# Feed-forward nets of a decoder trunk: gate, up and down by blocks with three matmuls a product, against two stages with two matmuls a product

## The chip, the cores and the metric

The kernel runs on one core of a Trainium2 chip. The metric is the time of one execution on the device in microseconds (us). Before the change the median of three runs is 920.85 us (920.54 to 921.05). The profiled execution spans 919.0 us from its first to its last instruction.

## What is computed

The reference is a decoder trunk in float32: 256 tokens of width 1024 go through two layers, each a feed-forward net (FFN), a mixer and another FFN. The even mixer is latent attention beside causal pooling, the odd one a gated spatial mixer.

```python
def _rmsnorm(x, g):
    xf = x.astype(jnp.float32)
    y = xf * lax.rsqrt(jnp.mean(xf * xf, axis=-1, keepdims=True) + EPS)
    return (y * g.astype(jnp.float32)).astype(x.dtype)

def _swiglu(x, w_gate, w_up, w_down):
    return (jax.nn.silu(x @ w_gate) * (x @ w_up)) @ w_down

...
    for layer in range(DEPTH):
        h = h + 0.5 * _swiglu(_rmsnorm(h, ffn_norm[layer, 0]), ffn_w_gate[layer, 0],
                              ffn_w_up[layer, 0], ffn_w_down[layer, 0])
        hn = _rmsnorm(h, mix_norm[layer])
...
        h = h + 0.5 * _swiglu(_rmsnorm(h, ffn_norm[layer, 1]), ffn_w_gate[layer, 1],
                              ffn_w_up[layer, 1], ffn_w_down[layer, 1])
```

The change concerns the four FFNs. Gate and up are 1024 x 2816 matrices, down is 2816 x 1024.

## The kernel before, in words

**Layout.** The residual `hT` lies with features on the partitions: 8 tiles of 128 features by 256 tokens. A product of an FFN is built with the weights as the stationary operand (128x128) and the 256 tokens moving.

**Split numbers.** TensorE multiplies in fp32r, so each float32 operand is split into a high half (rounded to fp32r) and a low half (the rest). A product takes three matmuls (`mm3`, lines 203 to 206): weights low times input high, weights high times input low, weights high times input high, all summed in one PSUM region. The input halves are two tiles, `xh` and `xl`; for the down projection they are `ph` and `pl`.

**Weight stream.** `chunks` lists all weights in the order of use, in pieces of 128 x 1024 floats (512 KB). SyncE (SP) loads each into a `raw` buffer (5 of them, line 157), ScalarE (ACT) casts it to `whi` (line 168), VectorE (DVE) subtracts to get `wlo` (line 176); there are 6 pairs of `whi` and `wlo`. `next_chunk` takes the next chunk and emits, ahead of the matmuls that use it, the casts and splits up to three chunks further on. All engines work their own instructions strictly in the order written here (a hand-written schedule), so what `next_chunk` emits stands on ACT and DVE behind everything emitted before it.

**An FFN (`ffn`, line 321).** The 2816 hidden features go in 11 blocks of 256. `gate_up(b)` uses four chunks of gate and up weights: for each of the 8 feature tiles k, four tiles of 128 outputs (two gate, two up), so 32 products of three matmuls. Two PSUM banks of 512 floats, G and U, hold two outputs each; they come from the rotating set of four `rot` banks. `epilogue` scales by the norm, applies Silu, multiplies, and splits the product into `ph` and `pl` (DVE lines 344, 347, 348, 352; ACT lines 345, 351). `down(b - 1)` then uses two chunks for the block before: 16 products, summed over all blocks into four `acc` banks that hold the eight output tiles of the FFN, two a bank. Gate/up of one block and down of the block before so alternate, six chunks a block.

**Norm.** The norm's factor is worked out beside the first block: `norm_sum` (a small matmul, then DVE line 275, then POOL, GpSimd) ahead of `gate_up(1)`, and `norm_row` (matmuls on lines 290 and 291, copies on lines 293 and 297) after two of its four chunks, followed by the epilogue of block 0.

**Handing over.** At a phase's end `finish` (line 305) adds each output tile to the residual (line 303, DVE), and makes the next phase's `xh` (line 253, ACT), `xl` (line 256, DVE) and squares (line 261, ACT; line 266, POOL). The next phase's matmuls begin as soon as the first of them is there.

**Extras in the first FFN.** After block 3 `early_loads` fetches small tensors; after block 6, behind the call of `down(5)`, `rope_tables` computes the rotary tables, about thirty small DVE instructions (lines 405 to 441) and one on ACT.

**The end.** In the last FFN the last two chunks go output tile by output tile, and each tile is added and sent out at once (line 395).

## Time and profile before

| what | value |
|---|---|
| median of the runs | 920.85 us |
| span of the profiled execution | 919.0 us |
| the profiled execution's own time | not listed apart from its span; the median of the runs lies 1.85 us above the span |
| TensorE matmuls | 7432, busy 909.8 us |
| VectorE busy | 577.4 us, 63% |
| ScalarE busy | 441.3 us, 48% |
| GpSimd busy | 96.9 us, 11% |
| read from HBM | 162.51 MB, 178 GB/s over the span |

The page gives busy time by engine, then the chain of work that ended last. In the rows of the timeline the first number is the start in us from the span's start, the second the duration. Matmuls are pipelined: a 128x256 matmul has a duration of 0.28 us, but the next one starts 0.12 us later, so what a matmul costs is the distance of the starts, not the duration. A row with "x4" merges four instructions, and a number in square brackets is the idle time of the engine ahead of it with what ended it.

### The profile page before, as it was taken

The page shows a single profiled execution, that of the slowest core. Times are in us where ns is not written, and L with a number is a line of the kernel's source. Part 1 is how long each engine was busy: PE and PEld are TensorE (multiplying, and loading weights), DVE is VectorE, ACT ScalarE, POOL GpSimd, SP SyncE. Part 2 cuts the span into 40 slices and gives each one's busy share as a digit, 9 for nine tenths or more (in the row PEclk, how much of TensorE's full clock was granted, in tenths as well). Part 3 has the DMA queues.
Part 4 walks back from the last instruction along what each step waited for, and adds up shares of the span by engine and source line. Part 5 has one row for each costly group of instructions (what it writes and reads, how often), then busy time and mean ns, then how long its engine had stood idle before and what let it go on. Part 6 is the DMA issues. An engine that isn't in the chain of part 4 may idle for free.

```text
span 919.0 us, 17791 instructions
## 1 busy us (share of the span) xinstructions
PE 909.8 (99%) x7432; PEld 899.8 (98%) x7432; DVE 577.4 (63%) x765; ACT 441.3 (48%) x606; POOL 96.9 (11%) x130
## 2 busy tenths in 40 slices
PE   8999999999999999999999999999999999999998
PEld 7999999999899999999999999999999999999998
DVE  7746576569876654654666654654858665564563
ACT  7535435457675543543554443543655554443441
POOL 4100000027523000000040000000220220000000
PEclk9999999999999999999999999999999999999999
DMA  8655645625353564464455464464446356356351
GB/s 279 230 194 192 223 139 192 222 103 178 111 165 117 198 226 172 157 227 167 160 208 184 151 234 166 154 229 168 151 176 204 126 196 245 143 186 226 139 183 47
DMA packets 48031, 164.70 MB, mean 179 GB/s; under 512 B 5456, under 2 KB 7760, under 8 KB 47952
## 3 DMA queue, kind: packets, MB, share of 16 engines
q1 hardware_dynamic: 47952, 163.58, 50.9%
q8 instruction: 58, 0.95, 0.4%
q14 instruction: 21, 0.17, 0.1%
HBM read 162.51 MB, written 1.05 MB: 178 GB/s over the span
## 4 chain that ended last, share of the span: by engine, by line
PE 96%; DVE 1%; POOL 1%; issue 1%; DMA 1%; SPq 0%; ACT 0%; DVEq 0%
PE rot L204 20%; PE rot L205 20%; PE rot L206 19%; PE acc L204 12%; PE acc L205 12%; PE acc L206 11%; DMA raw<-w_gu 1%; PE rot L942 0%; POOL diag L285 0%; DVE wlo L181 0%; PE rot L791 0%; PE rot L821 0%; PE acc L272 0%; PE rot L763 0%; DVE nb L800 0%
## 5 line engine op out<-in xcount | busy, mean ns | idle before, releaser
L204 PE MATMUL rot<-xh,wlo 128*128 128x256 f32 x1440 | 408.7, 284 | 1.8 <-DVE wlo L181 1.7
L205 PE MATMUL rot<-xl,whi 128*128 128x256 f32 x1440 | 407.3, 283 | 0.0
L206 PE MATMUL rot<-xh,whi 128*128 128x256 f32 x1440 | 407.2, 283 | 0.0
L168 ACT CAST whi<-raw 128x1024 fp32r<-128x1024 f32 (+2 forms) x303 | 305.6, 1044 | 177.9 <-PE rot L206 121.1
L176 DVE TENSOR_TENSOR wlo<-raw,whi 128x1024 fp32r<-128x1024 f32 (+2 forms) x298 | 350.2, 1226 | 42.1 <-ACT whi L168 41.9
L204 PEld LDWEIGHTS rot<-xh,wlo 128*128 128x128 f32 x1440 | 276.0, 192 | 2.9 <-DVE wlo L181 2.8
L205 PEld LDWEIGHTS rot<-xl,whi 128*128 128x128 f32 x1440 | 276.1, 192 | 0.0
L206 PEld LDWEIGHTS rot<-xh,whi 128*128 128x128 f32 x1440 | 276.0, 192 | 0.0
L204 PE MATMUL acc<-ph,wlo 128*128 128x256 f32 x704 | 198.0, 281 | 0.0
L205 PE MATMUL acc<-pl,whi 128*128 128x256 f32 x704 | 197.8, 281 | 0.0
L206 PE MATMUL acc<-ph,whi 128*128 128x256 f32 x704 | 197.6, 281 | 0.0
L344 DVE TENSOR_TENSOR t<-rot,rb 128x512 f32<-128x512 f32 x44 | 30.4, 690 | 193.9 <-PE rot L206 193.9
L206 PEld LDWEIGHTS acc<-ph,whi 128*128 128x128 f32 x704 | 132.8, 189 | 0.0
L205 PEld LDWEIGHTS acc<-pl,whi 128*128 128x128 f32 x704 | 132.8, 189 | 0.0
L204 PEld LDWEIGHTS acc<-ph,wlo 128*128 128x128 f32 x704 | 132.7, 188 | 0.0
L345 ACT ACTIVATE t<-t 128x512 f32<-128x512 f32 x44 | 27.8, 632 | 177.0 <-DVE t L344 177.0
L266 POOL TENSOR_TENSOR sqsum<-sq,sq 128x256 f32<-128x256 f32 x6 | 4.7, 778 | 529.6 <-ACT sq L261 529.6
L352 DVE TENSOR_TENSOR pl<-p,ph 128x512 fp32r<-128x512 f32 x44 | 30.5, 693 | 30.2 <-ACT ph L351 30.2
L351 ACT CAST ph<-p 128x512 fp32r<-128x512 f32 x44 | 27.3, 620 | 37.9 <-DVE p L348 37.9
L256 DVE SCALAR_TENSOR_TENSOR xl<-par_h,xh 128x256 fp32r<-128x256 f32 x48 | 30.4, 634 | 4.9 <-ACT xh L253 4.6
L348 DVE TENSOR_TENSOR p<-p,t 128x512 f32<-128x512 f32 x44 | 30.5, 693 | 4.8 <-ACT t L345 0.3
L253 ACT ACTIVATE xh<-par_h 128x256 fp32r<-128x256 f32 x48 | 24.3, 506 | 14.7 <-DVE par_h L303 11.6
(221 smaller groups left out, 748.5 us busy)
## 6 DMA issues: line engine op xcount, KB each, us to landing
raw<-w_gu SPq DMA_DIRECT2D x172, 512.0 KB, 4.8
raw<-w_down SPq DMA_DIRECT2D x88, 512.0 KB, 5.0
raw<-ew_out SPq DMA_DIRECT2D x8, 512.0 KB, 3.5
raw<-ow_v SPq DMA_DIRECT2D x8, 512.0 KB, 5.2
raw<-ow_u SPq DMA_DIRECT2D x8, 512.0 KB, 4.8
raw<-ow_out SPq DMA_DIRECT2D x8, 512.0 KB, 3.6
raw<-ew_p SPq DMA_DIRECT2D x4, 512.0 KB, 4.5
raw<-w_gu SPq DMA_DIRECT2D x7, 256.0 KB, 4.9
```

The source lines that it names most:

```text
L168: nc.scalar.copy(hi[:, :n], r[:, :n])
L176: eng.tensor_sub(lo[:, :n], r[:, :n], hi[:, :n].bitcast(F32))
L204: nc.tensor.matmul(out, wl, xh, start=start, stop=False, skip_group_check=True)
L205: nc.tensor.matmul(out, wh, xl, start=False, stop=False, skip_group_check=True)
L206: nc.tensor.matmul(out, wh, xh, start=False, stop=stop, skip_group_check=True)
L253: nc.scalar.activation(s.xh[:, k, :], hT[:, k, :], AF.Copy, scale=pcol(s.gname, s.goff + k))
L256: nc.vector.scalar_tensor_tensor(s.xl[:, k, :], hT[:, k, :], pcol(s.gname, s.goff + k), s.xh[:, k, :].bitcast(F32), op0=ALU.mult, op1=ALU. ...
L344: nc.vector.tensor_mul(t, bank3(G), bc(s.rb))
L345: nc.scalar.activation(t, t, AF.Silu)
L348: nc.vector.tensor_mul(p, p, t)
L351: nc.scalar.copy(ph, p)
L352: nc.vector.tensor_sub(pl, p, ph.bitcast(F32))
```

## The change

The weights of an FFN come in another order: all 44 chunks of gate and up, then all 22 of down. The FFN runs in two stages. The products of all blocks are kept in one SBUF tile `pp` (22 tiles of 128 features, low half and high half side by side).

The input's two halves lie side by side as well, in one tile `x`, low first. A product takes two matmuls (`mm2`): weights low times input high (256 columns), and weights high times both halves at once (512 columns). The result fills a whole bank of 512 floats: the first half holds the two small parts, the second the large one, and they have to be added afterwards.

`gate_up` therefore fills four banks a block instead of two; even blocks take the `acc` banks, odd ones the `rot` banks. A new step `evacuate` copies the first halves to SBUF (ACT) and adds the second halves (DVE), and `epilogue` works from SBUF. The down stage uses all eight banks, one for each output tile; the first three chunks are used for tiles 0 to 3 and then for 4 to 7, and the last two chunks go tile by tile in every FFN. Each tile is added to the residual in two steps (`add`), one for each half. The rotary tables are emitted behind `epilogue(6)`, as the code's order has it. The mixers still use three matmuls; their tiles only lie differently.

```diff
     def ffn_chunks(li):
         gu = [[w_gu[li, b, c] for c in range(4)] for b in range(NB)]
         dn = [[w_down[li, b, j] for j in range(2)] for b in range(NB)]
-        out = list(gu[0])
-        for b in range(1, NB):
-            out += gu[b] + dn[b - 1]
-        return out + dn[NB - 1]
+        return sum(gu, []) + sum(dn, [])
...
+    def mm2(bank, wh, wl, x, start, stop):
+        nc.tensor.matmul(bank[:, 0:T], wl, x[:, 1, :], start=start, stop=False, skip_group_check=True)
+        nc.tensor.matmul(bank, wh, x.rearrange("p s t -> p (s t)"), start=False, stop=stop,
+                         skip_group_check=True)
...
-        s.xh = xpool.tile([P, KD, T], F32R, tag="xh", name=nm("xh"), bufs=2)
-        s.xl = xpool.tile([P, KD, T], F32R, tag="xl", name=nm("xl"), bufs=2)
+        s.x = xpool.tile([P, KD, 2, T], F32R, tag="x", name=nm("x"), bufs=2)
+        s.xl, s.xh = s.x[:, :, 0, :], s.x[:, :, 1, :]
...
-    def finish(accs, nxt):
-        """h += acc; then the next phase's norm input."""
-        residual(accs, 0)
+    def finish(add, nxt):
+        add(0)
         for m in range(KD):
             norm_hi(nxt, m)
             if m + 1 < KD:
-                residual(accs, m + 1)
+                add(m + 1)
             norm_lo(nxt, m)
             norm_sq(nxt, m)
...
             def gate_up(b, hooks={}):
-                G, U = rot_bank(), rot_bank()
+                new = rot_bank if b % 2 else acc_bank
+                banks = [new() for _ in range(4)]
...
-                        for i, bank in enumerate((G, G, U, U)):
+                        for i, bank in enumerate(banks):
                             ms = slice(i * P, (i + 1) * P)
-                            mm3(bank3(bank)[:, i % 2, :], wh[:, kc, ms], wl[:, kc, ms],
-                                s.xh[:, k, :], s.xl[:, k, :],
-                                start=k == 0 and i % 2 == 0, stop=k == KD - 1)
-                return G, U
+                            mm2(bank, wh[:, kc, ms], wl[:, kc, ms], s.x[:, k], k == 0, k == KD - 1)
+                return banks
+
+            def evacuate(banks):
+                gu = fp.tile([P, 4, T], F32, tag="gu", name=nm("gu"))
+                a = fp.tile([P, 4, T], F32, tag="a", name=nm("a"), bufs=1)
+                for i, bank in enumerate(banks):
+                    nc.scalar.copy(a[:, i, :], bank[:, 0:T])
+                for i, bank in enumerate(banks):
+                    nc.vector.tensor_add(gu[:, i, :], bank[:, T:], a[:, i, :])
+                return gu
+
+            pp = fp.tile([P, 2 * NB, 2, T], F32R, tag="pp", name=nm("pp"), bufs=1)
...
-            gu0 = gate_up(0)
-            accs[0] = acc_bank()
+            gu0 = evacuate(gate_up(0))
+            bank = acc_bank()
...
             for b in range(1, NB):
-                gb = gate_up(b, {0: lambda: norm_sum(s, accs[0]), 2: mid} if b == 1 else {})
-                if b == 1:
-                    prev = later[0]
-                    for j in range(1, 4):
-                        accs[j] = acc_bank()
-                now = epilogue(*gb)
-                down(b - 1, *prev)
-                prev = now
+                gb = gate_up(b, {0: lambda: norm_sum(s, bank), 2: mid} if b == 1 else {})
+                epilogue(b, evacuate(gb))
                 if first and b == 3:
                     early_loads()
                 if first and b == 6:
                     rope_tables()
...
+            banks = [rot_bank() for _ in range(4)] + [acc_bank() for _ in range(4)]
+            K = 2 * NB
+
+            def down(k, m, w):
+                ms = slice(m * P, (m + 1) * P)
+                mm2(banks[m], w[0][:, 0, ms], w[1][:, 0, ms], pp[:, k], k == 0, k == K - 1)
+
+            def add(m):
+                for half in (banks[m][:, T:], banks[m][:, 0:T]):
+                    nc.vector.tensor_add(hT[:, m, :], half, hT[:, m, :])
+
+            ws = [next_chunk(1) for _ in range(3)]
+            for ms in (range(4), range(4, KD)):
+                for k in range(3):
+                    for m in ms:
+                        down(k, m, ws[k])
+            for k in range(3, K - 2):
+                w = next_chunk(1)
+                for m in range(KD):
+                    down(k, m, w)
+            ws = [next_chunk(1), next_chunk(1)]
+            for m in range(KD):
+                for j in range(2):
+                    down(K - 2 + j, m, ws[j])
+                if nxt is None:
+                    add(m)
+                    nc.sync.dma_start(outT[m], hT[:, m, :])
             if nxt is not None:
-                down(NB - 1, ph, pl)
-                finish(accs, nxt)
...
+                finish(add, nxt)
...
-            finish(accs, nxt)
+            finish(lambda m: residual(accs, m), nxt)
```

The first rows below are TensorE's (PE) at the start of FFN 1, where the even mixer's output projection ends and `gate_up(0)` begins, before the change. Names are out<-in with buffer numbers, then partitions x columns; `rot` and `acc` are PSUM banks; the words in brackets are the engines that the instruction waits for.

```order
L206 MATMUL acc_2877<-comb_h,whi_3165 128x256
L204 MATMUL rot_3482<-xh_2878,wlo_3249 128x256 [waits Activation_49]
L205 MATMUL rot_3482<-xl_2879,whi_3248 128x256 [waits DVE_49]
L206 MATMUL rot_3482<-xh_2878,whi_3248 128x256
L204 MATMUL rot_3482<-xh_2878,wlo_3249 128x256
L205 MATMUL rot_3482<-xl_2879,whi_3248 128x256
L206 MATMUL rot_3482<-xh_2878,whi_3248 128x256
L204 MATMUL rot_3483<-xh_2878,wlo_3249 128x256 [waits PE_49]
```

The same place on the same engine after the change:

```order
L203 MATMUL acc_2448<-comb,whi_2735 128x256
L207 MATMUL acc_3053<-x_2449,wlo_2819 128x256 [waits DVE_49,Activation_49]
L208 MATMUL acc_3053<-x_2449,whi_2818 128x512 [waits DVE_49]
L207 MATMUL acc_3054<-x_2449,wlo_2819 128x256 [waits DVE_49]
L208 MATMUL acc_3054<-x_2449,whi_2818 128x512
L207 MATMUL acc_3055<-x_2449,wlo_2819 128x256 [waits DVE_49]
L208 MATMUL acc_3055<-x_2449,whi_2818 128x512
L207 MATMUL acc_3056<-x_2449,wlo_2819 128x256 [waits DVE_49]
```

A product is now a 256 and a 512 wide matmul, and each of the four products of the first feature tile goes to an `acc` bank and waits for VectorE on its own, where before they went to `rot` banks and only the inputs were waited for.

The second place is VectorE (DVE) in the first FFN, where the rotary tables are computed. Before (`pl` is the last step of the epilogue of block 6, `wlo` the split of a weight chunk, `posi` the first step of the tables):

```order
L348 TENSOR_TENSOR p_1467<-p_1467,t_1464 128x512 [waits DVE_49,Activation_49]
L352 TENSOR_TENSOR pl_1471<-p_1467,ph_1470 128x512 [waits Activation_49]
L176 TENSOR_TENSOR wlo_1435<-raw_1316,whi_1434 128x1024 [waits DMAHW3_49]
L176 TENSOR_TENSOR wlo_1475<-raw_1348,whi_1474 128x1024 [waits DMAHW4_49,Activation_49]
L405 CAST posi_1534<-pos_i 128x2
```

After (`pp` is the last step of the epilogue of block 6):

```order
L355 TENSOR_TENSOR gu_987<-gu_987,rb_388 128x512 [waits DVE_49]
L357 TENSOR_TENSOR gu_987<-gu_987,rbh_390 128x512 [waits DVE_49]
L358 TENSOR_TENSOR gu_987<-gu_987 128x512 [waits DVE_49,Activation_49]
L361 TENSOR_TENSOR pp_212<-gu_987,pp_212 128x2x256 [waits Activation_49]
L419 CAST posi_1003<-pos_i 128x2
```

The two splits that stood between the epilogue and the tables are gone from there: the next split (`wlo_966`, the chunk of the last quarter of `gate_up(7)`) now stands behind the whole of the tables.

More of the change, by code (lines that the diff above doesn't have):

```diff
@@ L342, in epilogue @@
+            def epilogue(b, gu):
                 bc = lambda r: r.unsqueeze(1).to_broadcast([P, 2, T])
-                t = fp.tile([P, 2, T], F32, tag="t", name=nm("t"))
-                nc.vector.tensor_mul(t, bank3(G), bc(s.rb))
+                t, p = gu[:, 0:2, :], gu[:, 2:4, :]
+                nc.vector.tensor_mul(t, t, bc(s.rb))
                 nc.scalar.activation(t, t, AF.Silu)
-                p = fp.tile([P, 2, T], F32, tag="p", name=nm("p"))
-                nc.vector.tensor_mul(p, bank3(U), bc(s.rbh))
+                nc.vector.tensor_mul(p, p, bc(s.rbh))
@@ L348, in epilogue @@
                 nc.vector.tensor_mul(p, p, t)
-                ph = fp.tile([P, 2, T], F32R, tag="ph", name=nm("ph"))
-                pl = fp.tile([P, 2, T], F32R, tag="pl", name=nm("pl"))
-                nc.scalar.copy(ph, p)
-                nc.vector.tensor_sub(pl, p, ph.bitcast(F32))
-                return ph, pl
-            def down(b, ph, pl):
-                for j in range(2):
-                    w = next_chunk(1)
-                    for m in range(KD):
-                        out_tile(accs, m, w, (ph[:, j, :], pl[:, j, :]), b == 0 and j == 0,
-                                 b == NB - 1 and j == 1)
@@ L362, in ffn @@
-            gu0 = gate_up(0)
-            accs[0] = acc_bank()
-            later = []
+                out = pp[:, 2 * b : 2 * b + 2]
+                nc.scalar.copy(out[:, :, 1, :], p)
+                nc.vector.tensor_sub(out[:, :, 0, :], p, out[:, :, 1, :].bitcast(F32))
+            gu0 = evacuate(gate_up(0))
+            bank = acc_bank()
             def mid():
                 norm_row(s, half=True)
-                later.append(epilogue(*gu0))
-            prev = None
+                epilogue(0, gu0)
@@ L719, in even_mixer @@
             steps23 = window_sums((2, 3), nc.vector)
[L722 to L723 removed]
+            comb = xpool.tile([P, KD, 2, T], F32R, tag="x", name="comb", bufs=2)
+            cl, ch = comb[:, :, 0, :], comb[:, :, 1, :]
             def pool_mix(c, bank):
@@ L913, in odd_mixer @@
             u_sb = ot([P, KD, T], "u_sb")
-            zh = xpool.tile([P, KD, T], F32R, tag="xh", name="z_h", bufs=2)
-            zl = xpool.tile([P, KD, T], F32R, tag="xl", name="z_l", bufs=2)
+            zz = xpool.tile([P, KD, 2, T], F32R, tag="x", name="zz", bufs=2)
+            zl, zh = zz[:, :, 0, :], zz[:, :, 1, :]
             mixed, zs = {}, {}
@@ L981, in odd_mixer @@
             nxt = norm_begin(*nxt_args)
-            finish(accs, nxt)
+            finish(lambda m: residual(accs, m), nxt)
         return nxt
```

12 lines of the change are left out of this document (removed).

## The prediction

> **What bounds the kernel now.** I read the page's busy times and its chain first, then TensorE's waits, then long windows inside the four FFNs.
>
> ```profile
> PE 909.8 (99%) x7432; PEld 899.8 (98%) x7432; DVE 577.4 (63%) x765; ACT 441.3 (48%) x606; POOL 96.9 (11%) x130
> PE 96%; DVE 1%; POOL 1%; issue 1%; DMA 1%; SPq 0%; ACT 0%; DVEq 0%
> ```
>
> ```profile
> PE rot L204 <- DVE wlo L181: 1.7, 4, 0.7
> PE acc L290 <- POOL diag L285: 1.2, 1, 1.2
> ```
>
> ```profile
> 30.00:200.00 170.00, 170.00 (x1426) 170.00 (x1425) 104.53 (x139) 74.10 (x89) 1.66 (x2) 1.00 0.53 188
> 285.00:475.00 190.00, 190.00 (x1594) 190.00 (x1593) 114.22 (x128) 85.06 (x105) 10.28 (x14) 1.00 0.51 181
> 475.00:655.00 180.00, 180.00 (x1505) 179.76 (x1504) 105.07 (x117) 78.66 (x93) 6.00 (x9) 1.00 0.54 189
> 735.00:915.00 180.00, 180.00 (x1511) 180.00 (x1510) 102.43 (x114) 73.30 (x82) 4.70 (x7) 1.00 0.49 172
> ```
>
> TensorE (PE) is the chain, and it hardly waits. The windows' columns are length, then busy time and count for PE, weight loads, DVE, ACT and POOL, then the granted clock (1.00). In 720 us there are 6036 matmuls; some two in each window only straddle its edge, so 720/6028 = 119.4 ns a matmul of 256 columns. Whatever shortens the matmul stream shortens the kernel, and any wait on PE now lengthens it.
>
> **The pair against the triple.** A 512 wide matmul with its own weight load is in the trace twice: first and last of 96 in the odd mixer, first and last of 12 in the even one.
>
> ```profile
> 653.49 0.40 PE L204 MATMUL rot<-whi,xl 128*128 128x512 f32 x1
> 675.03 0.39 PE L206 MATMUL rot<-whi,xh 128*128 128x512 f32 x1
> ```
>
> ```profile
> 215.96 0.39 PE L204 MATMUL acc<-whi,ckvl 128*128 128x512 f32 x1
> 218.52 0.39 PE L206 MATMUL acc<-whi,ckvh 128*128 128x512 f32 x1
> ```
>
> 21.54/95 = 226.7 ns and 2.56/11 = 232.7 ns. I take 226.7: a long stream beside DMA, like the FFN's. Doubling the columns adds 107 ns, so about 12 ns of each matmul depend on no column, and the change drops one of three such parts: 3 x 119.4 = 358.3 becomes 119.4 + 226.7 = 346.1, 12.2 ns less (6.2 with 232.7). There are 4 x (352 + 176) = 2112 products. The first 48 lie where PE waits for others anyway (below), so 2064 x 12.2 = **25.2 us gained**, at the least 12.8.
>
> [...]
>
> **Work added beside PE.** A block of gate/up now has four copies on ACT and four adds on DVE more.
>
> ```profile
> 101.68 0.69 DVE L344 TENSOR_TENSOR t<-rot,rb 128x512 f32<-128x512 f32 x1 [5.57 <-PE rot L206]
> 105.19 5.76 DVE L176 TENSOR_TENSOR wlo<-raw,whi 128x1024 fp32r<-128x1024 f32 x5
> L303 DVE TENSOR_TENSOR par_h<-acc,par_h 128x256 f32<-128x256 f32 x48 | 19.6, 418 | 15.5 <-PE acc L206 15.5
> 481.89 0.37 ACT L293 COPY rb<-acc 128x256 f32<-128x256 f32 x1 [3.89 <-PE acc L291]
> raw<-w_gu SPq DMA_DIRECT2D x172, 512.0 KB, 4.8
> ```
>
> An epilogue takes 3.5 us (101.68 to 105.19), a split 1.15. From the end of a block's matmuls: last copy 0.6 us, adds to 1.05, epilogue to 4.6, four splits to 9.2. A block of PE is 32 x 0.346 = 11.1 us, so DVE has 1.9 us to spare. The first split behind the epilogue is done at 5.8 and needed after three chunks, at 8.3. On ACT the casts of the next chunks stand behind the copies and Silu, and begin at about 4.1; the first of them is wanted by the split at 5.8. SP issues a load when the split before it in that buffer is done, so four loads go out between 5.8 and 9.2 and land 4.8 us later; their casts come behind the next block's epilogue, after 15. So in the steady stage the extra work costs nothing; without the 1.9 us of cover, every microsecond more on DVE would cost PE one in each of 40 blocks (rival 2). At the start of down the twelve products on the `rot` banks (4.2 us) cover the evacuation of the `acc` banks. DMA moves the same bytes, and the number of splits is the same.
>
> **Rotary tables.** Here the cover is gone.
>
> ```profile
> 118.87 0.69 DVE L344 TENSOR_TENSOR t<-rot,rb 128x512 f32<-128x512 f32 x1 [5.57 <-PE rot L206]
> 122.37 2.35 DVE L176 TENSOR_TENSOR wlo<-raw,whi 128x1024 fp32r<-128x1024 f32 x2
> 124.64 0.16 DVE L405 CAST posi<-pos_i 128x2 f32<-128x2 int32 x1
> 130.79 4.62 DVE L176 TENSOR_TENSOR wlo<-raw,whi 128x1024 fp32r<-128x1024 f32 x4
> ```
>
> The tables hold DVE for 6.15 us (124.64 to 130.79). Before, two splits stood ahead of them. Now they follow epilogue 6 directly: 4.6 + 6.15 + 1.2 = 12.0 us until the split of the last chunk of gate_up(7) is done, and PE wants it at 8.3: **3.7 us lost**.
>
> **The banks at a phase's start.** `gate_up(0)` used to take `rot` banks, which were free. Its four `acc` banks are now those in which the phase before left its result, and each is free only when DVE has added it to the residual. After a mixer the last two tiles share a bank, so the fourth product waits for tile 7.
>
> ```profile
> 273.99 0.28 PE L204 MATMUL rot<-xh,wlo 128*128 128x256 f32 x1
> 277.71 0.41 DVE L303 TENSOR_TENSOR par_h<-acc,par_h 128x256 f32<-128x256 f32 x1
> 725.53 0.28 PE L204 MATMUL rot<-xh,wlo 128*128 128x256 f32 x1
> 729.24 0.41 DVE L303 TENSOR_TENSOR par_h<-acc,par_h 128x256 f32<-128x256 f32 x1
> ```
>
> The even mixer's tile 7 is added at 278.12; with 0.06 for the signal the fourth product ends at 278.53, against 273.99 + 4 x 0.346 = 275.37: 3.15 us. The odd one is the same (730.06 against 726.91): **6.3 us for the two**. Later feature tiles are ready by then.
>
> Between FFN 1 and FFN 2 each tile has its own bank and takes two adds, the second waiting for the first.
>
> ```profile
> 462.28 0.51 ACT L253 ACTIVATE xh<-par_h 128x256 fp32r<-128x256 f32 x1 [2.91 <-DVE par_h L303]
> 462.82 0.48 DVE L256 SCALAR_TENSOR_TENSOR xl<-par_h,xh 128x256 fp32r<-128x256 f32 x1 [0.25 <-ACT xh L253]
> 465.73 0.41 DVE L303 TENSOR_TENSOR par_h<-acc,par_h 128x256 f32<-128x256 f32 x1
> 466.06 0.63 DVE L256 SCALAR_TENSOR_TENSOR xl<-par_h,xh 128x256 fp32r<-128x256 f32 x1
> 466.61 0.41 DVE L303 TENSOR_TENSOR par_h<-acc,par_h 128x256 f32<-128x256 f32 x1
> ```
>
> Starts follow each other at 0.33 (add to `xl`) and 0.55 us (`xl` to add); a dependent add I put at 0.45 (0.42 and the signal; bounds 0.42 and 0.52). So 1.33 us a tile. Counted from the time tile 0 is summed, DVE has added tiles 4, 5, 6 and 7 at 5.55, 6.9, 8.25 and 9.6; PE, which by then runs tile by tile at 2 x 0.346, could begin the next FFN at 4.6. Its fourth product ends at 10.0 instead of 6.0: **4.0 us lost**. After FFN 0 and FFN 2 the mixers begin on the early `rot` banks; only a split behind the longer `finish` comes later.
>
> ```profile
> 206.71 0.43 PE L205 MATMUL rot<-wlo,xh 128*128 128x416 f32 x1
> ```
>
> That matmul already starts 0.27 us late in the even mixer; `finish` will end 6.1 instead of 5.6 us after the mixer's start: **0.5 us lost**.
>
> **The norm's wait, and the ends.**
>
> ```profile
> 18.09 1.75 DVE L176 TENSOR_TENSOR wlo<-raw,whi 128x1024 fp32r<-128x1024 f32 x1
> 20.30 0.16 DVE L275 TENSOR_SCALAR me<-acc 128x2 f32<-128x2 f32 x1 [0.46 <-PE acc L272]
> 27.37 0.39 PE L290 MATMUL acc<-diag,ones_r 128*128 128x256 f32 x1 [1.25 <-POOL diag L285]
> ```
>
> `norm_sum` now takes the bank of the first product of `gate_up(0)`, and L275 stands behind the four adds. In FFN 0 the split runs to 19.84, the adds follow, L275 moves from 20.3 to 21.2 and POOL's chain with it: L290 comes **0.9 us later**, and until there PE's gain is swallowed (the 48 products). In the other FFNs the same chain misses PE by some 0.15 us: **0.5 us for three**.
>
> ```profile
> 915.17 0.28 PE L206 MATMUL acc<-ph,whi 128*128 128x256 f32 x1
> 915.48 0.43 DVE L303 TENSOR_TENSOR par_h<-acc,par_h 128x256 f32<-128x256 f32 x1 [0.28 <-PE acc L206]
> ```
>
> At the very end the last add is done 0.45 us after PE. Two adds a tile (0.79) are slower than PE's 0.69 a tile, so DVE falls behind by 0.7 and has one add more: 1.55 us after PE, **1.1 us lost**.
>
> **The sum.** Lost: 3.7 + 6.3 + 4.0 + 0.5 + 0.9 + 0.5 + 1.1 = 17.0 us. Gained: 25.2. The span goes from 919.0 to 910.8; the median lies 1.85 above the span, so **912.6 us**, 0.9% faster. A measurement of this kernel can tell about 0.2% (1.8 us) from no change.
>
> **Rivals.**
>
> (1) *The wide matmul is dearer, slower than before.* If the 512 wide matmul beside the FFN's load costs what the twelve at 215.96 cost, the gain is 12.8, less 17.0: span 923.2, time 925.1. It turns at 25.2 - 17.0 = 8.2 us over 2064 products, 4.0 ns more than 226.7. For it: those twelve ran beside busy DVE, ACT and POOL. Against: the four windows run beside a busy DVE and ACT too and vary by less than 1 ns. Chance 0.14. [...]
>
> (2) *VectorE becomes the bound of gate/up.* If its block takes 11.5 us (operands that lie apart, waits for ACT), 0.4 us in each of 40 blocks is 16 us: 928.6. For it: only 1.9 of 11.1 us are spare. Against: all durations are those of the same shapes. Chance 0.08.
>
> (3) *The clock drops in the new pauses.* Should PE work at half speed for as long as a pause lasted (four pauses of some 3.7 us), it loses 4 x 1.85 = 7.4 us: 920.0. The windows grant 1.00, but show no such pause. Chance 0.06. [...]
>
> (4) *The pauses are shorter.* If PE's waits for the banks overlap with waits that I counted apart, or adds follow faster, and half of the 17.0 remains: 904.1. Chance 0.07.
>
> **Chances and range.** The forecast has 0.65; its own range, from the bounds of the dependent add and 1.5 ns either way on the pair, is 909 to 917. The range that should hold 8 in 10 takes in (3) and (4) in part and the near half of (1): 907 to 924. Faster by over 0.2%: the forecast, (4) and a little of (1): 0.73. Within 0.2%: the near edge of (1) and (3): 0.09. Slower: 0.18.
>
> **What would show it.** In the profile after: 256 and 512 wide matmuls following each other at 119 and 227 ns; PE waiting some 3.7 us for `wlo` once near 98 us (28.6 plus 25 chunks of 2.77); waits of the first products of FFN 1, 2 and 3 for L390 or L303 of 3 to 4 us in sum each; no wait of PE for `wlo` in other blocks. The forecast is wrong if the 512 wide matmul takes 231 ns or more, if PE waits in every block, or if the clock row falls below 1.00.

## The result, and the profile after

The changed kernel takes 927.61 us (median of 6 runs, 922.17 to 932.35) where the kernel before takes 920.64 beside it (6 runs, 920.11 to 921.05): ratio 1.008, 95% interval 1.0063 to 1.0098. It is 0.8% slower; 912.6 us, 0.9% faster, was forecast. The profiled execution took 928.45 us, its span is 926.3. One execution of an experiment below, e2_banks, took 3221.06 us at full clock; nothing on record says why, and it is left out of that median and range.

The head of the page after, with the granted clock in 40 slices and the chain:

```profile
span 926.3 us, 13892 instructions
PE 903.3 (98%) x5320; PEld 793.7 (86%) x5320; DVE 649.3 (70%) x973; ACT 498.2 (54%) x782; POOL 98.9 (11%) x130
PEclk9999999999998999999989999999999999999999
PE 88%; DVE 7%; POOL 1%; ACT 1%; issue 1%; DMA 1%; SPq 0%; DVEq 0%; POOLq 0%; ACTq 0%
```

There are 2112 matmuls fewer, as the change says, but PE is busy only 6.5 us less, and two slices of the clock row are no longer 9. What PE waited for (sum in us, times, longest; rows of under 0.4 us and three that are as before left out):

```profile
PE acc L207 <- DVE par_h L306: 4.5, 4, 1.1
PE rot L207 <- DVE wlo L173: 3.3, 1, 3.3
PE acc L207 <- DVE par_h L390: 3.1, 4, 0.9
PE acc L207 <- DVE wlo L178: 2.5, 4, 1.4
PE acc L293 <- POOL diag L288: 1.5, 1, 1.5
PE acc L275 <- DVE gu L347: 0.4, 1, 0.4
```

Three of them are new and are those that the prediction named: for the split behind the rotary tables (L173), for the mixers' results in the banks (L306), for FFN 1's results (L390). The waits for L178 all lie in the first 19 us, where the kernel before has 1.7 us of them. No block of the steady stage waits for VectorE. What was not forecast shows behind each wait. PE's rows at the end of the tables' pause:

```profile
101.38 0.58 PE L207 MATMUL rot<-x,wlo 128*128 128x256 f32 x1 [3.25 <-DVE wlo L173]
101.76 0.63 PE L208 MATMUL rot<-x,whi 128*128 128x512 f32 x1
102.40 0.63 PE L208 MATMUL rot<-x,whi 128*128 128x512 f32 x1
103.04 0.63 PE L208 MATMUL rot<-x,whi 128*128 128x512 f32 x1
103.68 0.63 PE L208 MATMUL rot<-x,whi 128*128 128x512 f32 x1
104.31 0.39 PE L208 MATMUL rot<-x,whi 128*128 128x512 f32 x1
```

Four pairs stand 0.64 us apart before they go back to 0.35. The windows there and behind the handing over to FFN 1 (columns as in the prediction; the granted clock is the third figure from the right):

```profile
101.00:102.00 1.00, 0.62 (x2) 0.62 (x3) 1.00 (x2) 1.00 (x2) 0.00 (x0) 0.50 0.00 0
103.00:104.00 1.00, 1.00 (x5) 0.90 (x4) 1.00 (x2) 0.00 (x0) 0.00 (x0) 0.50 1.07 381
105.00:106.00 1.00, 1.00 (x8) 0.88 (x7) 0.81 (x3) 1.00 (x4) 0.00 (x0) 1.00 0.93 352
277.00:278.00 1.00, 0.62 (x2) 0.30 (x2) 1.00 (x3) 0.94 (x3) 0.92 (x2) 1.00 0.00 0
279.00:280.00 1.00, 0.97 (x3) 0.87 (x4) 0.95 (x2) 0.99 (x3) 0.92 (x2) 0.50 0.00 0
284.00:285.00 1.00, 1.00 (x5) 0.81 (x5) 0.94 (x1) 0.00 (x0) 0.00 (x0) 0.50 0.83 336
286.00:287.00 1.00, 1.00 (x8) 0.88 (x7) 0.00 (x0) 0.35 (x1) 0.00 (x0) 1.00 0.96 373
```

The clock is 0.50 from 100.86 to 104.27 us behind the tables and from 278.35 to 285.17 behind the handing over, long after PE has work again. The same is seen at FFN 2 (469.49 to 476.32) and FFN 3 (735.74 to 739.15).

These edges, read from the granted clock of narrow windows, show when the clock falls. Its four falls, at 100.86, 278.35, 469.49 and 735.74 us, lie 177.49, 191.14 and 266.25 us apart, which is 52, 56 and 78 times 3.413 us; the half clock lasts 3.41 us behind the first and the last and 6.82 and 6.83 us behind the others, once and twice 3.413. So all eight edges of this execution lie on one grid of 3.413 us. These are the four grid windows that end with a fall (the second figure is PE's busy time in them):

```profile
97.44:100.86 3.42, 0.69 (x4) 0.32 (x3) 2.89 (x16) 2.28 (x4) 0.00 (x0) 1.00 0.00 0
274.94:278.35 3.41, 1.71 (x8) 0.75 (x6) 3.41 (x9) 3.25 (x9) 3.11 (x4) 1.00 0.11 41
466.08:469.49 3.41, 1.37 (x5) 0.59 (x4) 3.31 (x9) 2.20 (x6) 1.45 (x2) 1.00 0.00 0
732.32:735.74 3.42, 1.61 (x7) 0.65 (x5) 3.42 (x9) 3.26 (x9) 3.10 (x5) 1.00 0.00 0
```

PE was busy in them for 0.69 to 1.71 of 3.41 us, about half of the window at most.

The second surprise is the pair itself, a product's narrow and wide matmul; its spacing is the distance from one wide matmul's start to the next. Starts of wide matmuls in FFN 1, from gate/up and from down:

```profile
300.05 0.40 PE L208 MATMUL rot<-x,whi 128*128 128x512 f32 x1
379.78 0.40 PE L208 MATMUL acc<-x,whi 128*128 128x512 f32 x1
```

```profile
410.06 0.39 PE L208 MATMUL acc<-pp,whi 128*128 128x512 f32 x1
459.87 0.40 PE L208 MATMUL acc<-pp,whi 128*128 128x512 f32 x1
```

The first two are 230 pairs apart: 346.7 ns a pair. The other two are 141 apart: 353.3 ns. A pair has two spacings, and each stands unchanged through a stage or a large part of it. Both are means: the single steps alternate, 0.35 and 0.34 us in the first stretch, 0.35 and 0.36 in the second. Counted over all starts, 1148 pairs of this execution stand at 346.7 ns, 912 at 353.3, and 51 lie beside waits or at half clock (some expectations below count by whole stages, which gives 880 for the 912).

### The profile page after: what moved, and what is told of

Its sections match the earlier page's. It is cut to its first block, busy times and chain, and to the rows that moved or that the text cites. A ratio compares the mean times of both kernels' runs of the same rounds, so it can differ in the third digit from the quotient of the medians.

```text
span 926.3 us, 13892 instructions
## 1 busy us (share of the span) xinstructions
PE 903.3 (98%) x5320; PEld 793.7 (86%) x5320; DVE 649.3 (70%) x973; ACT 498.2 (54%) x782; POOL 98.9 (11%) x130
## 4 chain that ended last, share of the span: by engine, by line
PE 88%; DVE 7%; POOL 1%; ACT 1%; issue 1%; DMA 1%; SPq 0%; DVEq 0%; POOLq 0%; ACTq 0%
PE acc L208 27%; PE rot L208 24%; PE acc L207 14%; PE rot L207 12%; PE acc L202 2%; PE acc L201 2%; PE acc L203 2%; DVE par_h L390 2%; DVE x L259 2%; PE rot L202 1%; PE rot L203 1%; PE rot L201 1%; DMA raw<-w_gu 1%; DVE wlo L173 1%; DVE par_h L306 1%
## 5 line engine op out<-in xcount | busy, mean ns | idle before, releaser
L173 DVE TENSOR_TENSOR wlo<-raw,whi 128x1024 fp32r<-128x1024 f32 (+2 forms) x298 | 353.8, 1229 | 102.0 <-ACT whi L165 101.9
L208 PE MATMUL acc<-x,whi 128*128 128x512 f32 x768 | 275.3, 401 | 0.0
L207 PE MATMUL acc<-x,wlo 128*128 128x256 f32 x768 | 219.0, 285 | 10.4 <-DVE par_h L306 4.5
L208 PE MATMUL rot<-x,whi 128*128 128x512 f32 x640 | 225.4, 396 | 0.0
L207 PE MATMUL rot<-x,wlo 128*128 128x256 f32 x640 | 179.3, 280 | 3.3 <-DVE wlo L173 3.3
L208 PEld LDWEIGHTS acc<-x,whi 128*128 128x128 f32 x768 | 147.5, 192 | 34.0
L207 PEld LDWEIGHTS acc<-x,wlo 128*128 128x128 f32 x768 | 148.0, 193 | 15.1 <-DVE par_h L306 6.7
L208 PEld LDWEIGHTS rot<-x,whi 128*128 128x128 f32 x640 | 120.7, 189 | 28.2
L208 PE MATMUL acc<-pp,whi 128*128 128x512 f32 x352 | 127.3, 396 | 0.0
L208 PE MATMUL rot<-pp,whi 128*128 128x512 f32 x352 | 127.3, 396 | 0.0
L207 PEld LDWEIGHTS rot<-x,wlo 128*128 128x128 f32 x640 | 121.1, 189 | 3.6 <-DVE wlo L173 3.6
```

Source lines behind the costliest of these rows:

```text
L173: eng.tensor_sub(lo[:, :n], r[:, :n], hi[:, :n].bitcast(F32))
L207: nc.tensor.matmul(bank[:, 0:T], wl, x[:, 1, :], start=start, stop=False, skip_group_check=True)
L208: nc.tensor.matmul(bank, wh, x.rearrange("p s t -> p (s t)"), start=False, stop=stop, skip_group_check=True)
```

## The experiments

Theory: the waits are worth what was forecast; the rest is (a) half clock outlasting four pauses and (b) pairs at 353.3 ns. Rivals: the pauses alone cost more than they were priced at; the wide matmul is dear by what runs beside it. Where matmuls of zeros are added, they are extra work. A kernel is set against the kernel before on the same chip (median 920.17 to 920.46 there).

### One pause moved: e1_tables

```diff
-                if first and b == 6:
-                    rope_tables()
...
+                if first and k == 8:
+                    rope_tables()
```

The second place is in the down loop, where DVE has time (it is busy for 24.14 of the 50 us from 145 to 195 us in the changed kernel).

> The changed kernel, with the rotary tables emitted behind the ninth chunk of the first FFN's down stage instead of behind the epilogue of block 6. Theory (pauses and the clock they bring down): the pause of 3.4 us near 98 us and the stretch of half clock behind it (2.7 us at half speed, 1.4 us lost) both go, so about 5 us less than the changed kernel: some 922 to 923 us, and three stretches of half clock remain. Rival (the low clock is not the pauses' doing): only the 3.4 us go and a stretch of half clock remains near 100 us: 924 us.

Measured: 921.77 us (919.46 to 926.22), ratio 1.0018 (1.0007 to 1.003). The wait for L173 is gone, the clock stays at 1.00 there, and the other waits and their three stretches of half clock stay (the mean clock is 0.992):

```profile
PE acc L207 <- DVE par_h L306: 4.5, 4, 1.1
PE acc L207 <- DVE par_h L388: 3.1, 4, 0.9
```

The median is 5.8 us below the changed kernel's, where the pause was priced at 3.7; the half clock behind it (four pairs 0.29 us late, 1.2) would go with it. As the runs of this kernel scatter by 7 us and those of the changed kernel by 10, this alone proves no size.

### The banks: e2_banks, e3_both

```diff
-                new = rot_bank if b % 2 else acc_bank
+                new = acc_bank if b % 2 else rot_bank
-            bank = acc_bank()
+            bank = rot_bank()
-            for ms in (range(4), range(4, KD)):
+            for ms in (range(4, KD), range(4)):
```

e2_banks has this alone, so `gate_up(0)` starts on the banks that are free early; e3_both has it and the moved tables.

> The changed kernel with the two sets of banks exchanged: even blocks of gate/up take the rotating banks, odd ones the accumulator banks, and the first three chunks of down go to tiles 4 to 7 first. At the start of FFN 1, 2 and 3 the first block's banks are then free. Theory (pauses and the clock they bring down): the three handover pauses (3.15 + 4.0 + 3.15 us) and the three stretches of half clock behind them (7 us lost) go: some 17 us less than the changed kernel, 910 to 911 us. Rival (the low clock is not the pauses' doing): only some 10 us go, 917 us, with half clock still at the start of the FFNs. Second rival (VectorE is late anyway, since the residual takes two adds a tile): PE waits for the inputs instead of the banks and less than 5 us go.

> The changed kernel with both edits, tables in the down stage and banks exchanged. Theory (pauses and the clock they bring down): 22 us less than the changed kernel, 905 to 906 us, which beats the kernel before by 15 us; the granted clock is 1.00 throughout and the runs agree with each other as closely as those of the kernel before. If the products that cost 353 instead of 347 ns do so because of the pauses ahead of them, 6 us more go: 899 us. Rival (the wide matmul is dearer beside this load): the pauses go but the pairs get dearer, and no more than 10 us are won.

Measured: e2_banks 915.30 us (911.81 to 916.22), ratio 0.9938 (0.9924 to 0.9953). That is some 5 us above its theory and near the rival's 917, but not for the rival's reason: the clock falls behind the tables alone and no longer at FFN 1, 2 and 3 (its mean is 0.998), while some 1570 pairs stand at 353.3 ns where the changed kernel had 912, which is 4.3 us more. e3_both 911.57 us (911.19 to 913.71), ratio 0.9909 (0.9896 to 0.9922), faster than both kernels. PE's three longest waits in e3_both (that for L178 is again at the kernel's start):

```profile
PE rot L207 <- DVE wlo L178: 1.5, 2, 1.2
PE rot L293 <- POOL diag L288: 1.5, 1, 1.5
PE rot L275 <- DVE gu L347: 1.4, 2, 0.9
```

The new waits are gone and the clock is 1.000. It is still some 6 us above what was expected of it, and the pairs say why: 1728 of them stand at 353.3 ns, only 366 at 346.7. What was gained at the waits was partly lost in the pairs.

### The clock by itself: e4_fill

```diff
+            def busy(bank, n):
+                for _ in range(n):
+                    nc.tensor.matmul(bank[:, 0:T], wu[:, 0:P], wu, start=True, stop=True)
...
+                            if k == 0 and pause[i]:
+                                busy(spare, pause[i])
```

The waits stay, but matmuls of zeros keep PE busy in them (28 in the tables' pause, 22, 35 and 22 at the three handings over).

> The changed kernel with its four pauses left as they are, but filled with matmuls on a constant tile into a free bank (28 in the pause near 98 us, 22, 35 and 22 at the starts of FFN 1, 2 and 3), which the results do not use. The waits for VectorE stay as long as they are. Theory (a pause brings the clock down and the half clock outlasts it): the granted clock stays at 1.00 or nearly, and about 8 us go though no wait is shortened: 919 to 920 us. Rival (the clock falls for another reason, such as the wide matmuls): the stretches of half clock stay and the time is the same or some us longer, 927 to 930 us.

Measured: 920.72 us (917.56 to 925.66), ratio 1.0012 (0.9996 to 1.0028). Two of the windows that had half clock:

```profile
103.00:104.00 1.00, 1.00 (x8) 0.88 (x7) 1.00 (x2) 1.00 (x4) 0.00 (x0) 1.00 0.93 332
284.00:285.00 1.00, 1.00 (x8) 0.88 (x8) 0.00 (x0) 0.00 (x0) 0.00 (x0) 1.00 0.66 250
```

With more work on PE and no wait shortened, the kernel is 6.9 us faster. The profiled execution took 920.55 us with 998 pairs at 353.3; against the 928.45 and 912 of the changed kernel that is 7.9 + 86 x 0.0066 = 8.5 us. Of these 0.7 lie ahead of all four pauses (the matmul on L293 starts at 28.29 us in the changed kernel's execution and at 27.62 in this one), so about 7.8 us are left for the half clock. Place by place the sum is the same: the 40 pairs across and behind each pause take 1.3, 2.8, 2.3 and 1.3 us less here, 7.7 in all. The pauses alone cannot explain this; the rival falls. But at a clock of 1.00 the runs still scatter by 8 us.

### The pair by itself: e5_three

```diff
-        nc.tensor.matmul(bank, wh, x.rearrange("p s t -> p (s t)"), start=False, stop=stop,
-                         skip_group_check=True)
+        nc.tensor.matmul(bank[:, 0:T], wh, x[:, 0, :], start=False, stop=False, skip_group_check=True)
+        nc.tensor.matmul(bank[:, T:], wh, x[:, 1, :], start=False, stop=stop, skip_group_check=True)
```

> The kernel with both edits (tables and banks), but with each product's wide matmul cut into its two halves again: three matmuls of 256 columns into the same two-half banks, all else the same. Its difference from the kernel with both edits, 911.6 us, is the worth of the wide matmul alone. The pairs theory (a pair costs 347.1 ns in one of the eight stages and 353.2 in the other seven there, against 358.1 for three starts in a row in the kernel before): 352 x 11.0 + 1760 x 4.9 = 12.5 us, so 924.1. The prediction's 12.2 ns for each of 2112 products: 25.8 us, so 937.4. A third theory, that the three matmuls also come cheaper in this arrangement (353 ns): no difference, about 912. The spacing of three starts is to be 358 ns in every stage by the first two.

Measured: 923.47 us (923.18 to 923.55), 11.9 above e3_both, where 12.5 was expected and the prediction's price gave 25.8. Starts of a triple's first matmul:

```profile
299.87 0.28 PE L207 MATMUL rot<-x,wlo 128*128 128x256 f32 x1
379.79 0.28 PE L207 MATMUL acc<-x,wlo 128*128 128x256 f32 x1
```

222 triples in 79.92 us: 360.0 ns (355 in the down stages; the kernel before has the same two, 358.1 in the mean). The triples have no second spacing within a stage, and the runs lie within 0.4 us.

### What sets the spacing: e6_kick, e7_rev, e8_again

e6_kick puts a small matmul ahead of the first product of each block but the first (it came to 40 of them, of 16 to 88 columns, since a stage has eleven blocks; the expectation counts 28):

```diff
+                        if k == 0 and b:
+                            n = 8 * (b + 1)
+                            nc.tensor.matmul(banks[0][:, 0:n], wu[:, 0:P], wu[:, 0:n], start=True, stop=True)
```

e7_rev turns the order in a product round, the wide matmul first:

```diff
-        nc.tensor.matmul(bank[:, 0:T], wl, x[:, 1, :], start=start, stop=False, skip_group_check=True)
-        nc.tensor.matmul(bank, wh, x.rearrange("p s t -> p (s t)"), start=False, stop=stop,
+        nc.tensor.matmul(bank, wh, x.rearrange("p s t -> p (s t)"), start=start, stop=False,
                          skip_group_check=True)
+        nc.tensor.matmul(bank[:, 0:T], wl, x[:, 1, :], start=False, stop=stop, skip_group_check=True)
```

e8_again is e3_both without any edit.

> The kernel with both edits, with one small matmul of zeros (bf16, 24, 32, 40, 48, 56, 64 or 72... columns: 8 more in each block, from 16 at the second block of a gate and up stage) ahead of the first product of each block but the first, into the bank that this product then starts afresh: 28 small matmuls of 0.01 to 0.05 us each, under 1.5 us in all. Theory A, that the spacing of a pair (346.7 or 353.3 ns) is a rhythm between the matmul and the weight load under it that locks in where a run of pairs starts and stays until something breaks it: the kicks break it, so blocks of one stage no longer share one spacing, and where the two spacings share the stages half and half the time is about 911.6 + 1.5 - 5 = 908. Theory B, that a stage's addresses or its transfers set the spacing: every stage keeps one spacing through, 353.3 in most, and the time is 911.6 to 913.1.

> The kernel with both edits, with the order in a product turned round: the matmul of 512 columns (high half of the weights) first, the one of 256 (low half) second. The stream of matmuls alternates as before, 256, 512, 256, 512, only a bank's last matmul is now the narrow one. If the alternation alone sets the two spacings, they are again 346.7 and 353.3 ns and the time lies between 899.5 (all at 346.7: 1760 x 6.5 ns less) and 912.8 (all at 353.3). If the change of bank between a wide and a narrow matmul costs the extra 6.6 ns, one spacing alone is seen, and the time is one end or the other.

> The kernel with both edits once more, unchanged, for a second profiled execution. If what sets the spacing is in the program (addresses, order, sizes), the same seven stages stand at 353.3 ns and the first at 347. If it locks in by the moment at which a stage starts, other stages may be at 346.7 in this execution, and the time differs by up to 352 x 6.6 ns = 2.3 us for a gate and up stage and 176 x 6.6 ns = 1.2 us for a down stage.

Measured: e6_kick 915.94 us (915.70 to 916.59), e7_rev 913.11 (910.32 to 913.92), e8_again 914.95 (one run). In e8_again the first stage, at 347 in e3_both, stands at 353: same program, other spacing. So it is not the addresses or the order of the program alone. e7_rev has 2009 pairs at 353.3 and lies just above the upper end of its expectation, 912.8, where one spacing alone would put it; as e8_again has 2045 without the edit, this tells nothing of the order. e6_kick missed the 908 of its theory A: a small matmul costs about 0.1 us where 0.01 to 0.05 was expected, and only 8 of the 40 blocks went to 347. But it shows the switch. First and last wide matmul of the blocks behind the kicks of 56 and of 64 columns in FFN 1:

```profile
342.14 0.39 PE L208 MATMUL rot<-x,whi 128*128 128x512 f32 x1
353.08 0.40 PE L208 MATMUL rot<-x,whi 128*128 128x512 f32 x1
353.32 0.20 PE L338 MATMUL acc<-wu 128*128 128x64 bf16 x1
353.56 0.40 PE L208 MATMUL acc<-x,whi 128*128 128x512 f32 x1
364.32 0.39 PE L208 MATMUL acc<-x,whi 128*128 128x512 f32 x1
```

31 pairs in 10.94 us (353 ns), and after one small matmul 31 in 10.76 (347 ns). In all four FFNs the eighth and the tenth block (64 and 80 columns) are at 347 ns and the blocks behind 24 to 56, 72 and 88 columns at 353. The blocks of one stage stand beside the same kinds of loads, casts and splits, so the rival of the neighbours' work falls: the spacing changed at a small matmul and then stood through the block (31 pairs). That it is a rhythm between the matmul and the weight load, as theory A has it, was the author's explanation and is not shown. The blocks ahead matter too. The kicks of 64 and 80 columns came behind a block at 353, those of 72 and 88 behind one at 347, so each of these four sizes turned the spacing over; the sizes up to 56 left 353 or brought it.

### Locking it: e9_lock, e10_lock48, e11_lock_after

```diff
+                        if k == 0 and b == 2:
+                            kick(banks[0])
...
+            kick(banks[4])
```

`kick` is the small matmul, of 64 columns in e9_lock and of 48 in e10_lock48, both on e3_both; the second one stands at the start of down. e11_lock_after has 64 columns in the changed kernel, with one more at the ninth block of the first FFN.

> The kernel with both edits, with eight small matmuls of zeros of 64 columns: one ahead of the third block of each gate and up stage and one ahead of the first product of each down stage, each into the bank that the next product starts afresh. In the kernel with 40 of them, those of 64 and 80 columns were followed by 347 ns a pair in all four FFNs, those of the other sizes by 353. Theory (the spacing is a rhythm that locks in where a run of pairs starts, and the size of what stands ahead decides it): all blocks from the third on and all down stages stand at 347; against all at 353.3 (914.95 in the second look at the kernel with both edits) that is 4 x (288 + 176) x 6.6 ns = 12.2 us less, and eight matmuls of 0.13 us more: about 903 to 904. Rival (those two sizes fell well by the place at which they stood, the eighth and tenth block): no better than 912 to 916.

> The same eight small matmuls with 48 columns in place of 64: as many instructions at the same places, 0.007 us shorter each. By the theory the size decides: 48 columns were followed by 353 ns in all four FFNs, so all stages stand at 353.3, about 914 to 916. If any small matmul there is as good, the time is that of the kernel with 64 columns, 903 to 904.

> The changed kernel itself, with nothing else altered than nine small matmuls of 64 columns: at the third block of each gate and up stage, at the ninth of the first FFN (behind the pause for the tables) and at the start of each down stage. Its pauses and the half clock behind them stay. By the account of the changed kernel (880 of its 2112 pairs at 353.3 in the profiled execution), it comes 880 x 6.6 ns = 5.8 us lower than that execution's 928.45, less 9 x 0.13 us for the small matmuls: 923 to 924, and the spread of its runs, 922.2 to 932.4 before, shrinks to about 1 us. If the spacing is no cause of the spread, time and spread stay: median about 927.6.

Measured: e9_lock 905.33 us (904.37 to 906.51), ratio 0.9838 (0.9826 to 0.9851), the fastest version of all: 1593 pairs at 346.7. Only FFN 2's gate/up went to 353. e10_lock48 914.43 us (914.23 to 914.65): 2024 pairs at 353.3. At the same places, then, the size makes 9.1 us. It does not decide alone, as the theory had it: FFN 2's gate/up was the only one that stood at 347 ahead of its kick of 64, and it was turned to 353, while 48 was followed by 353 whatever stood ahead.

e11_lock_after 925.69 us (918.50 to 929.27), ratio 1.0051 (1.0031 to 1.0072): the scatter did not shrink, and that expectation fell. Its profiled execution took 918.5 us with 225 pairs at 353.3, and these are windows at the tables' pause and, last, at FFN 2's handing over:

```profile
99.00:100.00 1.00, 0.00 (x0) 0.00 (x0) 0.97 (x5) 1.00 (x3) 0.00 (x0) 1.00 0.00 0
101.00:102.00 1.00, 1.00 (x8) 0.86 (x7) 1.00 (x2) 0.91 (x1) 0.00 (x0) 1.00 0.39 111
469.00:470.00 1.00, 1.00 (x5) 0.90 (x4) 1.00 (x1) 0.50 (x1) 0.56 (x1) 0.50 0.01 4
```

The same pause (3.28 us) left the clock at 1.00 here; of the four only FFN 2's was followed by half clock. The grid of 3.413 us, counted back from that fall at 464.42 us, shows what differs: a grid line falls into the tables' pause and shares it between two windows.

```profile
95.78:99.19 3.41, 1.61 (x9) 1.13 (x8) 2.76 (x17) 1.32 (x3) 0.00 (x0) 1.00 0.00 0
99.19:102.60 3.41, 1.93 (x11) 1.71 (x12) 3.40 (x5) 2.72 (x3) 0.00 (x0) 1.00 0.28 86
```

PE is busy for 1.61 and 1.93 us in them, where the changed kernel's execution had one window with 0.69. At FFN 1 and FFN 3 it is 2.14 to 2.30 us here and the clock stays; at FFN 2 it is 1.45 and the clock falls. The limit is not sharp by these figures (1.61 us was followed by a fall at the changed kernel's FFN 3), but in these two executions the grid lay differently against the tables' pause, with 0.69 us of work in the window ahead of the fall and with 1.61 and 1.93 us where the clock stayed.

The mean clock of the runs and their time go together: 926.55 to 929.27 us at 0.986 to 0.989, 923.54 to 924.84 at 0.992 to 0.994, 918.50 and 918.87 at 0.995. So half clock behind these pauses is a matter of the execution, and it makes the scatter together with the pairs.

### Both at once: e12_fill_lock, e13_fill_set, e14_set

e12_fill_lock joins e4_fill with 14 kicks of 64 columns; e13_fill_set joins it with kicks of 48 and, two products later, 64; e14_set has these on e3_both:

```diff
+                            if k == 0 and i in (0, 2) and (b == 2 or first and b == 8):
+                                kick(bank, 48 if i == 0 else 64)
...
+                if k == 0 and m in (1, 3):
+                    kick(banks[m], 48 if m == 1 else 64)
```

> The changed kernel with its four pauses filled with dummy matmuls (clock at 1.00, pauses as long as they were) and with fourteen small matmuls of 64 columns that lock the spacing of the pairs: at the third and fifth block of each gate and up stage, the ninth and tenth of the first FFN, and the start of each down stage. By the account (waits as predicted, half clock 8.4 us, pairs at 353.3 in place of 346.7): the profiled execution with the pauses filled, 920.55 us, had 1056 pairs at 352.5 to 353.3, so 1056 x 6.4 = 6.7 us less, and 14 x 0.125 = 1.8 us for the small matmuls: 915.6, of which 1.8 are the experiment's own, so 913.9 beside the 912.6 that was predicted; and a spread of runs under 2.5 us, where the fill alone had 917.6 to 925.7 and the locking alone 918.5 to 929.3. If something else makes the runs differ, the spread stays at 7 us or more, and the median near 920.

> The changed kernel with its four pauses filled with dummy matmuls (clock at 1.00) and the spacing of the pairs set by two small matmuls, one of 48 columns (behind it 353 in every case so far) and two products later one of 64 (turns 353 into 347): at the third block of each gate and up stage, the ninth of the first FFN, and at the second and fourth product of each down stage; 18 small matmuls. Theory: from each such place to the stage's end all pairs at 347, in every execution. From the fill's profiled execution (920.55 us, 998 pairs at 353): the two first blocks of a stage stay as they fall (4 x 64 pairs, half of them at 353: 128), so 870 x 6.6 = 5.7 us less, and 18 x 0.125 = 2.2 us more: 917.0, within 1.5 either way; without the 2.2 of the experiment itself 914.8, beside 912.6 predicted. Rival, that something else than clock and spacing keeps the changed kernel's time up or makes its runs differ: all pairs at 347 but 920 or more, or runs that lie 5 us and more apart.

> The kernel with both edits (no pauses) with the same setting: 48, then two products later 64 columns, at the third block of each gate and up stage and the second and fourth product of each down stage, 16 small matmuls. The version with eight of 64 columns alone had 495 pairs at 353 in its profiled execution of 904.65 us, most of them in one gate and up stage that its small matmul turned the wrong way. With the setting at most the two first blocks of each stage are left, about 128 pairs: 367 x 6.6 = 2.4 us less and 8 x 0.125 = 1.0 more: 903.2. If the setting does not hold, 908 to 915.

Measured: e12_fill_lock 922.89 us (921.31 to 925.78), e13_fill_set 922.48 (921.01 to 924.51), e14_set 909.63 (909.13 to 910.00). All three missed, because the spacing could not be set: in e12_fill_lock the third block's kick turned three FFNs from 353 to 347 and the fifth block's turned them back; in e13_fill_set and e14_set all eight down stages went to 353 and six of eight gate/up stages to 347. Inside gate/up a single kick of 64 at a block's start turned the spacing over in all 23 cases of e6, e9, e11 and e12 (16 times from 353 to 347, 7 times back). At the start of down the same kick was followed by 347 in all four stages of e9 and e11 and by 353 in three of e12, so no rule for it is shown. What the count of pairs is worth, these misses show all the better. From each family's first execution, with 6.6 ns for a pair more at 353.3 and 0.125 us for a kick (the pair of starts across one is 0.48 us in place of 0.35):

| profiled execution | pairs at 353.3 | kicks | worked out, us | measured, us |
|---|---|---|---|---|
| e3_both | 1728 | 0 | start | 911.94 |
| e7_rev | 2009 | 0 | 913.8 | 913.92 |
| e8_again | 2045 | 0 | 914.0 | 914.95 |
| e6_kick | 1776 | 40 | 917.3 | 915.70 |
| e9_lock | 495 | 8 | 904.8 | 904.65 |
| e10_lock48 | 2024 | 8 | 914.9 | 914.23 |
| e14_set | 1145 | 16 | 910.1 | 909.58 |
| e4_fill | 998 | 0 | start | 920.55 |
| e12_fill_lock | 1406 | 14 | 925.0 | 924.67 |
| e13_fill_set | 921 | 18 | 922.3 | 921.79 |

Over 10 us of time follow from the count within 1 us, save e6_kick with its many kicks. A run of the changed kernel with full clock and nearly all pairs at 346.7 was not reached.

## Why the prediction was wrong

**The waits: right.** The account of the changed kernel's span: 919.0, less what its pairs gain (1148 x 11.4 ns, 912 x 4.8 ns and about 0.5 us for the 51 others: 18.0 us against 358.1 ns a triple), plus 7.8 us of half clock from e4_fill. To reach 926.3, 17.5 us are left for the waits; 17.0 was predicted. Term by term: at the tables the step from one wide matmul to the next is 4.03 us where a pair takes 0.35, 3.7 lost, 0.15 of it by the clock (3.7 predicted). At FFN 1 the first four wide matmuls start like this:

```profile
275.02 0.39 PE L208 MATMUL acc<-x,whi 128*128 128x512 f32 x1
275.77 0.40 PE L208 MATMUL acc<-x,whi 128*128 128x512 f32 x1
277.52 0.39 PE L208 MATMUL acc<-x,whi 128*128 128x512 f32 x1
279.42 0.63 PE L208 MATMUL acc<-x,whi 128*128 128x512 f32 x1
```

4.40 us for three steps of 0.35: 3.35 lost, 0.15 of it by the clock (3.15 predicted); FFN 3 has the same 4.40. At FFN 2 the steps from FFN 1's last wide matmul through FFN 2's first four are 1.50, 1.54, 1.42 and 1.53 us: 4.6 lost (4.0 predicted; 4.4 with the clock held in e4_fill). The chain of the norm in FFN 0 ends 0.9 us later than before (L293 at 28.29 against L290 at 27.37), as predicted, though e4_fill's execution, with the same chain, has it at 27.62. e3_both bears the terms out from the other side: against e4_fill's execution it saves 920.55 - 911.94 = 8.6 us, and 4.8 more that its 730 additional pairs at 353.3 hide: 13.4 for the tables and the three handings over, priced at 14.0, less the 1.0 that PE waits longer for L275 there (1.4 in place of 0.4).

**The step "I take 226.7" failed.** The prediction had both values in its rows, 226.7 and 232.7 ns, and put the difference down to what ran beside the matmul. The FFN's pairs take either price, stage by stage and beside the same work: 346.7 and 353.3 ns, less the 119.4 of a narrow matmul, are 227.3 and 233.9. Whether the twelve at 232.7 take the same two prices is not shown; no run changed them. The gain was 18.0 us in the profiled execution in place of 25.2; the rest, 7.2, is for the most part rival (1) for 912 of 2112 pairs (6.0 us of it). Its argument against that rival, that the four windows vary by less than 1 ns, spoke of triples, which e5_three shows to have no second spacing within a stage.

**"Should PE work at half speed" was made a rival where it was a term.** It was given 0.06 and 7.4 us; it came, and cost 7.8. The clock did come down at the pauses, as the rival stated. The kernel before has a granted clock of 1.00 throughout its span; half speed for as long as a pause lasted was the author's estimate. The changed kernel's windows show 0.50. What was wrong is the rival's weight: each of four pauses was forecast at 3 to 4 us, and nothing in the trace spoke for a clock that would stay. The price was near by luck, since the half clock did not last as long as its pause: 3.41 us behind the tables and FFN 3's handing over, 6.82 and 6.83 behind FFN 1's and FFN 2's, with PE still waiting in part of them. In the traces the clock changed on a grid of 3.413 us, and at the tables a pause of 3.25 us ended at 0.50 in the changed kernel's execution and one of 3.28 us at 1.00 in e11_lock_after's. A long wait was not needed: at FFN 1 no single wait was longer than 1.12 us, PE was busy for 1.71 us of the window of 3.41, and the clock fell.

**Rivals (2) and (4).** VectorE did not become the bound: no steady block waits for it, though it is 72 us busier. The pauses were not shorter.

The forecast's sum was 912.6; 7.2 us of pairs and 7.8 of clock more make 927.6, and the profiled execution took 928.45. Of the 0.8 us between, 0.3 are the execution's distance from its span (2.15 us where 1.85 was taken) and 0.5 the waits.

## What to carry to other kernels

Here four new pauses in a stream that PE bounds cost more than their own length: 7.8 us of half clock came on top, behind windows of 3.41 us in which PE was busy for 0.69 to 1.71 us. Where a change opens such pauses, ask what the clock does behind them and price it as a term, and close the pauses (other banks, side work moved to where its engine has time) before judging the change. When two rows give two prices for one instruction, find out whether both can occur in the stage in question before taking one. The changed kernel's runs scattered by 10 us where those of the kernel before scattered by 1; its mean clock went from 0.988 to 0.995, and the first stage of e3_both's program stood at 347 ns a pair in one execution and at 353 in the next. What so varies between executions has to be counted in each profile before medians are compared.

## What the hardware showed that was not expected

- A run of alternating 256 and 512 column matmuls, each with its own weight load (5320 of each on the page after), stood at 346.7 or at 353.3 ns a pair. It kept one of them over long stretches (230 and 141 pairs in the rows of FFN 1 above) and differed between executions of one program (347 in the first stage of e3_both, 353 in e8_again). Inside gate/up one small matmul of 64 columns turned it over in 23 of 23 cases, while behind one of 48 it stood at 353.3 in all four such blocks of e6_kick and every stage of e10_lock48. What sets the spacing stays open; no run here took the weight load apart from the matmul.
- The granted clock changed on a grid of 3.413 us: all eight edges of the changed kernel's profiled execution lie on it. It fell at the end of grid windows in which PE was busy for 0.69 to 1.71 us (1.45 in e11_lock_after) and held behind windows with 1.61 us and more in e11_lock_after, so no sharp limit is shown. It then stayed at 0.50 for 3.41 us or about 6.83. The grid lay differently against the program in the two executions: the tables' pause cost half clock in the one (3.25 us) and none in the other (3.28 us).
